# Attention of two blocks: the transposes of a block two steps after its scores, its values three steps after, and six score buffers in place of four

## The chip, the cores and the metric

The kernel runs on one core of a Trainium2 chip. The metric is the device time of one execution in microseconds (us). The engines are named as the profile names them: PE (TensorE, matmuls; PEld is its weight load), DVE (VectorE), ACT (ScalarE), POOL (GpSimd), SP (SyncE, which issues most transfers). L512 is line 512 of the kernel.

## What is computed

Two blocks of two layers each on 512 tokens of width 1024, all in float32. The change lies in the attention of the first layer of either block; the rest (a mixture of experts, a state space mixer, convolutional feed-forward layers) is left as it is. Cut to the two attentions:

```python
def chunk_attention(q, k, v, rel_bias):          # first block, 8 heads of 64
    ...
    scores = jnp.einsum('bclhd,bcshd->bchls', q, k_band).astype(jnp.float32) * (ATT_HEAD_DIM ** -0.5)
    scores = scores + bias[None, None]
    scores = jnp.where(valid[None, :, None, None, :], scores, -1e30)
    p = jax.nn.softmax(scores, axis=-1).astype(v.dtype)
    o = jnp.einsum('bchls,bcshd->bclhd', p, v_band)

def fox_attention(q, k, v, f_logit, q_gain, k_gain):   # second block, 8 heads of 64
    ...
    s = jnp.einsum('bqhd,bkhd->bhqk', qi, k).astype(jnp.float32) * scale
    s = s + ci.transpose(0, 2, 1)[..., None] - ck[:, :, None, :]
    s = jnp.where(kpos[None, :] <= pi[:, None], s, NEG_INF)
    pr = jax.nn.softmax(s, axis=-1)
    return jnp.einsum('bhqk,bkhd->bqhd', pr.astype(v.dtype), v)
```

## The kernel before

Activations lie with channels on the 128 partitions and the 512 tokens along the free axis. A linear layer of 1024 x 128 weights (`lin`, L253) is 24 matmuls of 128x512, since every operand is split into a high and a low part and three products are kept (L268, L269, L270). `flowing` (L308) issues such a layer in two halves of 12 matmuls with a `yield` between; between the halves the kernel puts other matmuls, so that PE has work while the other engines are busy with a softmax. Weights come through SP into `w`; ACT casts them to `wh` (L223), DVE takes the difference `wl` (L224), two buffers each.

Attention is done for a pair of heads at a time, four pairs per block, by the generator `attend` (L501). The queries are cut into four blocks of 128 tokens; block i has 128(i+1) keys.

- `scores(i, h)` (L508): one matmul into a bank of `pa` (two buffers; L512); DVE adds the bias and keeps the maximum (L517), ACT takes the exponential and its sum (L521), DVE takes the reciprocal and scales the row (L522, L523). The result is the tile `S`.
- `turned(i, h)` (L525): i+1 transposes of `S` by PE into a bank of `pm` (L530); ACT copies them to the tile `PT` (L532).
- `values(i)` (L534): 2(i+1) matmuls of `PT` with the values `vt` into `po` (one buffer; L538).

One step of `attend` holds the scores of block j for both heads, then the values of block j-2, then the transposes of block j-1, and a `yield`. There are six steps.

PE's instructions stand in the order in which they are written (a manual schedule); the other engines' order is set by a scheduler that places each instruction by its own estimate. `pm` has two buffers in all, and besides the transposes of `S` they serve the transposes of the value rows (`v_rows`, L494, L498, copied to `vt` by DVE at L499), those of the norms of q and k (`heads`, L1896), the sums of squares (L1882), and in the gated units L1951, whose bank DVE reads at L1959.

In the first block (`mixer0`, L556) a pair's projections v, k, q give six halves, and after each of them one step of the pair before is run; whatever is left is run at the end of the pair (`drain`, L654), before the next pair's first half. At the same time DVE reduces the rows of the modulation weights (`ada`, L419; L441, 128x1024 each), whose tiles `we` SP loads. In the second block (`mixer2`, L1789) `heads` has two steps, in the second of which the first step of `attend` runs, and then one step after each half of the following projections; a pair that is not finished goes on beside the next pair or, for the last one, beside the gated units (`gated`, L1938; `spatial`, L1964). DVE there also computes factors for a later layer (`s5_factors`, L1397; L1407).

Of the kernel before, what the change touches and what calls it, by code (L numbers as in the profile page):

```python
# [17 lines left out]
T = 512  # L18
# [122 lines left out]
def _build(ctx, tc, A, out, dbg, upto, cap):  # L141
    nc = tc.nc
    V, S, G, PE = nc.vector, nc.scalar, nc.gpsimd, nc.tensor
# [10 lines left out]
    def tl(p, shape, tag, bufs=1, dt=F32):  # L154
        return p.tile(list(shape), dt, name=tag, tag=tag, bufs=bufs)
# [6 lines left out]
    def ps_(tag="ps", bufs=3):  # L162
        return tl(pp if tag in ("ps", "pm") else phase["px"], [128, T], tag, bufs)
# [337 lines left out]
    def attend(ap, c, q):  # L501

        qT, kT, vt = q["q"], q["k"], q["vt"]
        sm, pts = {}, {}

        def scores(i, h):  # L508
            w = 128 * (i + 1)
            pb = 64 * h  # L510
            sp = ps_("pa", 2)
            PE.matmul(sp[:, :w], qT[pb:pb + 64, i * 128:w], kT[pb:pb + 64, :w], start=True, stop=True)  # L512
            s = sm[i, h] = tl(ap, [128, T], "S", 4)
            m = tl(ap, [128, 4], "m", 8)
            prev = -3e38
            for n, (c0, c1, b) in enumerate(q["bias"][h](i)):
                V.tensor_tensor_reduce(s[:, c0:c1], sp[:, c0:c1], b, 1.0, prev, op0=ADD, op1=MAX,  # L517
                                       accum_out=m[:, n:n + 1])
                prev = m[:, n:n + 1]
            V.tensor_scalar(m[:, 2:3], prev, -1.0, None, op0=MUL)  # L520
            S.activation(s[:, :w], s[:, :w], AF.Exp, bias=m[:, 2:3], accum_out=m[:, 3:4])  # L521
            V.reciprocal(m[:, 3:4], m[:, 3:4])  # L522
            V.tensor_scalar(s[:, :w], s[:, :w], m[:, 3:4], None, op0=MUL)  # L523

        def turned(i, h):  # L525
            w = 128 * (i + 1)
            s = sm.pop((i, h))
            tp = ps_("pm", 2)
            for j in range(i + 1):
                PE.transpose(tp[:, j * 128:(j + 1) * 128], s[:, j * 128:(j + 1) * 128], ident)  # L530
            pt = pts[i, h] = tl(ap, [128, T], "PT", 4)
            S.activation(pt[:, :w], tp[:, :w], AF.Copy)  # L532

        def values(i):  # L534
            for j in range(i + 1):
                for h in range(2):
                    f = (2 * c + h) * 64
                    PE.matmul(q["o"][64 * h:64 * h + 64, i * 128:(i + 1) * 128], vt[:, j, f:f + 64],  # L538
                              pts[i, h][:, j * 128:(j + 1) * 128], start=(j == 0), stop=(j == i))

        for j in range(6):
            for h in range(2):
                if j < 4:
                    scores(j, h)
            if j == 2:
                q["o"] = ps_("po", 1)
            if j >= 2:
                values(j - 2)
            for h in range(2):
                if 1 <= j < 5:  # L550
                    turned(j - 1, h)
            yield


# [1 line left out]
    def mixer0(rb, mp):  # L556
        with ExitStack() as st:
# [84 lines left out]
            for c in range(5):  # L642
                q = {"vt": vt}
                lins = inner(c, q) if c < 4 else project(0)
                if c < 4:
                    biases(c, q)
                for n, _ in enumerate(lins):
                    if att:
                        step(att)
                    if c == 0 and n < 4:  # L650
                        pooled(n)
                    step(aw, 2 if n % 3 == 0 else 1)
                if att:
                    drain(att)  # L654
                    mixed[3 + c] = hl(op, 16, old["o"])
                if c < 4:
                    att, old = attend(ap, c, q), q
# [1131 lines left out]
    def mixer2(sp, hf):  # L1789

        with ExitStack() as st:
# [98 lines left out]
            def heads(c, q):  # L1890
# [12 lines left out]
                for h in (2 * c, 2 * c + 1):  # L1903
# [10 lines left out]
                    q["bias"].append(bias)  # L1914
                yield
                att = attend(ap, c, q)
                next(att)
                v_rows(q["v"], vt, c)
# [209 lines left out]
```

## Time and profile before

| | |
|---|---|
| median of 3 runs | 2448.61 us (2448.13 to 2453.47) |
| the profiled execution | 2448.66 us, its span 2446.9 us |
| PE, DVE, ACT busy | 95%, 72%, 45% of the span |
| `attend` in the first block | 85.8 to 191.8 us |
| `attend` in the second block | 1228.1 to 1353.3 us |
| transposes L530, values L538 in all | 160 and 320 matmuls |

PE is busy nearly always, so what a stage can win is read from PE's idle time there and from the clock that was granted, not from the shares of the whole span. A row of PE gives the modelled duration of a matmul, which is longer than the distance to the next start, since matmuls are pipelined.

### The profile page before, as it was taken

What the parts mean: (1) busy time and instruction counts of PE and PEld (TensorE: products, weight loads), DVE (VectorE), ACT (ScalarE), POOL (GpSimd) and SP (SyncE); (2) the same over time, 40 slices, a digit from 0 to 9 for tenths busy, and PEclk for the clock granted to TensorE, in tenths of its full rate; (3) what the DMA queues carried; (4) which work ended last, traced back from release to release, by engine and by line L of the source; (5) the groups of instructions that cost most, each with busy time, mean ns of one, the idle gap of its engine ahead of it and who ended that gap; (6) DMA issues with size and microseconds to landing.
All of it is one profiled execution on the core that took longest, in us unless ns stands there. A gap on an engine that the chain in (4) does not pass through costs nothing.

```text
span 2446.9 us, 35789 instructions
## 1 busy us (share of the span) xinstructions
PE 2328.9 (95%) x13173; PEld 1906.3 (78%) x13174; DVE 1750.3 (72%) x3323; ACT 1096.4 (45%) x1750; POOL 486.6 (20%) x498
## 2 busy tenths in 40 slices
PE   7999899899999999999999999999998799999999
PEld 4767799677777776998766777778787788888887
DVE  6985678699996885776686687647847756745755
ACT  3444787434433434885245434324333244423432
POOL 0000444100000002343010394676521000000000
PEclk9999999899999999999899999999999999999999
DMA  9862898553354225896221233343347733323242
GB/s 343 290 214 92 285 334 281 179 186 124 113 165 145 87 77 182 289 338 236 75 70 62 84 118 112 104 132 112 103 129 236 205 106 95 95 84 108 95 126 95
DMA packets 136789, 385.94 MB, mean 158 GB/s; under 512 B 24696, under 2 KB 41208, under 8 KB 134560
## 3 DMA queue, kind: packets, MB, share of 16 engines
q1 hardware_dynamic: 121408, 338.51, 42.0%
q0 software_dynamic: 7552, 26.74, 3.2%
q10 hardware_dynamic: 7648, 18.32, 2.2%
q8 instruction: 108, 1.77, 0.3%
q14 instruction: 73, 0.60, 0.1%
HBM read 354.13 MB, written 29.38 MB: 157 GB/s over the span
## 4 chain that ended last, share of the span: by engine, by line
PE 43%; DVE 7%; ACT 1%; issue 1%; DMA 0%; SPq 0%; POOL 0%; ACTq 0%; DVEq 0%; POOLq 0%
PE ps L268 13%; PE ps L270 13%; PE ps L269 13%; DVE wl L224 2%; DVE hc L2016 1%; ACT wh L223 1%; PE pm L372 0%; PE sk L1590 0%; PE pa L512 0%; DMA w<-w_d 0%; PE pm L530 0%; PE py L1715 0%; PE po L538 0%; DVE hc L2020 0%; PE pm L1580 0%
## 5 line engine op out<-in xcount | busy, mean ns | idle before, releaser
L268 PE MATMUL ps<-hi,wh 128*128 128x512 f32 (+2 forms) x2248 | 899.7, 400 | 4.0 <-ACT hi L485 3.2
L270 PE MATMUL ps<-hi,wl 128*128 128x512 f32 (+2 forms) x2248 | 885.8, 394 | 8.8 <-DVE wl L224 8.8
L269 PE MATMUL ps<-lo,wh 128*128 128x512 f32 (+2 forms) x2248 | 885.6, 394 | 3.7 <-DVE lo L486 2.7
L223 ACT ACTIVATE wh<-w 128x1024 fp32r<-128x1024 f32 (+3 forms) x323 | 306.9, 950 | 572.9 <-PE ps L269 384.6
L224 DVE TENSOR_TENSOR wl<-w,wh 128x1024 fp32r<-128x1024 f32 (+3 forms) x323 | 370.6, 1147 | 215.8 <-ACT wh L223 211.7
L270 PEld LDWEIGHTS ps<-hi,wl 128*128 128x128 f32 (+1 forms) x2248 | 425.3, 189 | 110.1 <-DVE wl L224 13.7
L268 PEld LDWEIGHTS ps<-hi,wh 128*128 128x128 f32 (+1 forms) x2248 | 425.8, 189 | 106.9 <-issue 12.4
L269 PEld LDWEIGHTS ps<-lo,wh 128*128 128x128 f32 (+1 forms) x2248 | 426.1, 190 | 96.0 <-DVE lo L486 4.0
L224 DVE TENSOR_TENSOR wl<-we,wh 128x1024 fp32r<-128x1024 f32 x128 | 173.9, 1373 | 59.9 <-ACT wh L223 55.2
L931 POOL TENSOR_TENSOR hl<-hT,hh 128x1024 fp32r<-128x1024 f32 x60 | 137.1, 2284 | 174.5 <-ACT hh L930 80.9
L223 ACT ACTIVATE wh<-we 128x1024 fp32r<-128x1024 f32 x128 | 136.0, 1064 | 48.7 <-PE pa L949 21.5
L2016 DVE SCALAR_TENSOR_TENSOR hc<-f,cols,hc 128x511 f32<-128x511 f32 (+1 forms) x176 | 152.4, 866 | 6.5 <-ACT hc L2014 3.1
L911 PE MATMUL ps<-ht,w 128*128 128x128 f32 x1024 | 125.7, 276 | 5.1 <-ACT ht L961 5.1
L911 PEld LDWEIGHTS ps<-ht,w 128*128 128x128 f32 x1024 | 119.4, 191 | 7.0 <-ACT ht L961 6.9
L734 POOL IOTA io<- 128x512 f32 x2 | 1.1, 564 | 574.9 <-PE ps L270 574.9
L2012 DVE TENSOR_TENSOR f<-ps,rb 128x512 f32<-128x512 f32 x88 | 60.5, 687 | 68.6 <-PE ps L270 68.3
L441 DVE CUSTOM_DVE_ANT_0 we<-we,crow 128x1024 f32<-128x1024 f32 x80 | 96.5, 1215 | 3.7 <-DMA we<-in_ada_t_dram 3.3
L949 PE MATMUL pa<-wh,hh 128*128 128x256 f32 x496 | 88.4, 300 | 1.0 <-ACT hh L930 1.0
L223 ACT ACTIVATE hi<-hc 128x512 fp32r<-128x512 f32 x44 | 27.8, 632 | 127.7 <-DVE hc L2020 127.7
L491 DVE SCALAR_TENSOR_TENSOR x<-ps,mod,x 128x512 f32<-128x512 f32 x52 | 39.0, 749 | 60.3 <-PE ps L270 50.1
L949 PE MATMUL pa<-wh,hl 128*128 128x256 f32 x496 | 78.8, 280 | 1.4 <-DVE hl L931 1.4
L949 PE MATMUL pa<-wl,hh 128*128 128x256 f32 x496 | 78.6, 280 | 0.0
(571 smaller groups left out, 3252.0 us busy)
## 6 DMA issues: line engine op xcount, KB each, us to landing
we<-in_w_ex_dram SPq DMA_DIRECT2D x128, 512.0 KB, 5.8
w<-in_w_fu_dram SPq DMA_DIRECT2D x88, 512.0 KB, 3.5
we<-in_ada_t_dram SPq DMA_DIRECT2D x80, 512.0 KB, 5.1
w<-in_w_ex_dram SPq DMA_DIRECT2D x64, 512.0 KB, 5.6
w<-in_w_si_dram SPq DMA_DIRECT2D x48, 512.0 KB, 3.5
w<-in_w_fd_dram SPq DMA_DIRECT2D x32, 512.0 KB, 3.7
w<-in_w_ei_dram SPq DMA_DIRECT2D x20, 512.0 KB, 3.5
aw<-in_ada_w_dram SPq DMA_DIRECT2D x16, 512.0 KB, 9.4
```

The source lines that it names most:

```text
L223: S.activation(hi, src, AF.Copy)
L224: eng.tensor_tensor(lo, src, hi.bitcast(F32), op=SUB)
L268: PE.matmul(ps[:m], a, h, start=(not more and k + j == 0), stop=False)
L269: PE.matmul(ps[:m], a, l, start=False, stop=False)
L270: PE.matmul(ps[:m], b, h, start=False, stop=(last and k + j == nk - 1))
L441: V.tensor_tensor_reduce(w, w, row, 1.0, 0.0, op0=MUL, op1=ADD, accum_out=st[:, n:n + 1])
L491: V.scalar_tensor_tensor(xs[c], ps, mod(l, seg, c), xs[c], op0=MUL, op1=ADD)
L911: PE.matmul(p[:, c * 128:(c + 1) * 128], w2[:, (4 * q + c) * 128:(4 * q + c + 1) * 128], hd, start=True, stop=True)
L931: (V if e < 2 else G).tensor_tensor(hl_, win, hh.bitcast(F32), op=SUB)
L949: PE.matmul(hp[:, 0:256], h[:, 4 * n + k], w[:, k * 256:(k + 1) * 256], start=(n + i + k == 0), stop=(n + i + k == 6))
L2012: V.tensor_tensor(t, next(up)[1], rb, op=MUL)
L2016: V.scalar_tensor_tensor(c[:, d:], t[:, :T - d], C(f"fw{l}{2 - d}", n), c[:, d:], op0=MUL, op1=ADD)
```

## The change

The number of `S` buffers goes from four to six. A step of `attend` now holds the scores of block j, the values of block j-3 and the transposes of block j-2, and there are seven steps.

```diff
@@ -510,7 +510,7 @@
             pb = 64 * h
             sp = ps_("pa", 2)
             PE.matmul(sp[:, :w], qT[pb:pb + 64, i * 128:w], kT[pb:pb + 64, :w], start=True, stop=True)
-            s = sm[i, h] = tl(ap, [128, T], "S", 4)
+            s = sm[i, h] = tl(ap, [128, T], "S", 6)
             m = tl(ap, [128, 4], "m", 8)
@@ -538,17 +538,17 @@
-        for j in range(6):
+        for j in range(7):
             for h in range(2):
                 if j < 4:
                     scores(j, h)
-            if j == 2:
+            if j == 3:
                 q["o"] = ps_("po", 1)
-            if j >= 2:
-                values(j - 2)
+            if j >= 3:
+                values(j - 3)
             for h in range(2):
-                if 1 <= j < 5:
-                    turned(j - 1, h)
+                if 2 <= j < 6:
+                    turned(j - 2, h)
             yield
```

PE in `mixer0`, at the end of the first pair (the same for the second and third): the values of block 2 (L538 x6), the transposes of block 3 (L530 x8), and then a half of a projection. Before:

```order
L538 MATMUL po<-PT,vt 64x128 x6
L530 MATMUL pm<-ident,S 128x128 x8
L268 MATMUL ps<-hi,wh 128x512
L269 MATMUL ps<-lo,wh 128x512
L270 MATMUL ps<-hi,wl 128x512
```

With the change, at the same place:

```order
L270 MATMUL ps<-hi,wl 128x512
L538 MATMUL po<-PT,vt 64x128 x6
L530 MATMUL pm<-ident,S 128x128 x8
L538 MATMUL po<-PT,vt 64x128 x8
L268 MATMUL ps<-hi,wh 128x512
```

Before, the twelve matmuls of a half stood between the transposes of block 3 and its values (L538 x8); now the values follow the transposes directly, because `mixer0` has six halves for seven steps.

PE in `mixer2`, at the end of the second pair (the same at the first and third): the next pair's transposes of its norms (`ye`, L1896) come in the same step.

```order
 L538 MATMUL po<-PT,vt 64x128 x6
 L530 MATMUL pm<-ident,S 128x128 x8
+L1896 MATMUL pm<-ident,ye 128x128 x8
 L268 MATMUL ps<-hi,wh 128x512
 L269 MATMUL ps<-lo,wh 128x512
```

Before, L1896 stood a half later, behind the values of block 3; now it follows the transposes of block 3, which fill both banks of `pm`.

PE in `mixer2`, beside the second gated unit: the transposes L1951 now stand ahead of the fourth pair's values of block 2 and transposes of block 3.

```order
+L268 MATMUL ps<-hi,wh 128x512
+L269 MATMUL ps<-lo,wh 128x512
+L270 MATMUL ps<-hi,wl 128x512
+L1951 MATMUL pm<-ident,f 128x128 x4
 L538 MATMUL po<-PT,vt 64x128 x6
 L530 MATMUL pm<-ident,S 128x128 x8
```

L1951 stood ahead of the values of block 3 before; so a bank of `pm` is now held by the gated unit while block 3 is transposed.

## Rows read from the trace of the kernel before

**Rows 1.** The page, busy time, share of the span, instructions of each engine.

```profile
PE 2328.9 (95%) x13173; PEld 1906.3 (78%) x13174; DVE 1750.3 (72%) x3323; ACT 1096.4 (45%) x1750; POOL 486.6 (20%) x498
```

**Rows 2.** Busy time by stretch: PE, PEld, DVE, ACT, POOL; then PE's clock, DMA share, GB/s.

```profile
110.00:140.00 30.00, 28.87 (x173) 20.48 (x173) 27.58 (x75) 15.34 (x34) 0.00 (x0) 1.00 0.91 322
1240.00:1270.00 30.00, 27.61 (x171) 20.62 (x171) 27.64 (x143) 12.86 (x28) 2.97 (x2) 0.99 0.20 57
...
1228.00:1353.00 125.00, 115.92 (x687) 86.26 (x688) 95.64 (x394) 62.62 (x143) 12.43 (x12) 0.97 0.22 68
```

**Rows 3.** Waits of PE in the first block's attention: total, times, longest.

```profile
PE pm L530 <- DVE mod L407: 1.0, 1, 1.0
PE pm L530 <- DVE S L523: 1.0, 1, 1.0
PE pm L530 <- DVE vt L499: 0.5, 1, 0.5
```

**Rows 4.** DVE in the first block: its waits for transfers, and two copies to `vt`.

```profile
DVE we L441 <- DMA we<-in_ada_t_dram: 2.8, 4, 2.0
...
122.41 0.67 DVE L499 COPY vt<-pm 128x512 f32<-128x512 f32 x1
...
151.29 0.68 DVE L499 COPY vt<-pm 128x512 f32<-128x512 f32 x1
```

**Rows 5.** Timeline of PE, end of the first pair: start, duration, what, idle before.

```profile
105.16 0.63 PE L530 MATMUL pm<-ident,S 128*128 128x128 f32 x4
106.76 0.63 PE L530 MATMUL pm<-ident,S 128*128 128x128 f32 x4 [0.97 <-DVE mod L407]
...
110.11 1.09 PE L538 MATMUL po<-PT,vt 128*64 128x128 f32 x16
```

**Rows 6.** Timeline of ACT at the same place.

```profile
105.89 0.60 ACT L532 ACTIVATE PT<-pm 128x512 f32<-128x512 f32 x1 [2.11 <-PE pm L530]
...
109.98 1.06 ACT L223 ACTIVATE wh<-w 128x1024 fp32r<-128x1024 f32 x1 [1.90 <-PE ps L269]
110.95 0.58 ACT L622 ACTIVATE q<-ps 128x512 f32<-128x512 f32 x1
```

**Rows 7.** Waits of PE in the second block's attention.

```profile
PE pm L530 <- DVE m L520: 1.9, 3, 1.0
...
PE po L538 <- ACT PT L532: 1.6, 2, 0.8
PE pm L530 <- DVE m L522: 1.5, 2, 0.8
PE pa L512 <- DVE qk L1899: 1.4, 1, 1.4
PE pa L512 <- DVE m L517: 1.4, 2, 0.7
PE pm L530 <- DVE S L523: 1.1, 2, 0.7
```

**Rows 8.** Timeline of PE: eight transposes L1896, and what follows them.

```profile
1257.93 1.09 PE L1896 MATMUL pm<-ident,ye 128*128 128x128 f32 x8
1258.78 0.47 PE L268 MATMUL ps<-hi,wh 128*128 128x512 f32 x1
```

**Rows 9.** Timeline of PE at two places where its clock falls.

```profile
1237.15 0.63 PE L268 MATMUL ps<-hi,wh 128*128 128x512 f32 x1
...
1331.34 0.33 PE L530 MATMUL pm<-ident,S 128*128 128x128 f32 x1 [0.99 <-DVE m L520]
...
1332.21 0.39 PE L268 MATMUL ps<-hi,wh 128*128 128x512 f32 x1
1332.44 0.40 PE L269 MATMUL ps<-lo,wh 128*128 128x512 f32 x1
...
1333.05 0.63 PE L268 MATMUL ps<-hi,wh 128*128 128x512 f32 x1
1333.48 0.63 PE L269 MATMUL ps<-lo,wh 128*128 128x512 f32 x1
```

## The prediction

> **What bounds the kernel now.** I read the page's busy times first: PE is busy 95% of the span, DVE 72%, ACT 45% [rows 1]. So a stage gives back only what PE idles in it, or runs at half clock. The busy times by stretch show the same inside the two attentions: in 110 to 140 us (first block) PE is busy 28.9 of 30 us at a granted clock of 1.00; in 1240 to 1270 us (second block) 27.6 of 30 at 0.99, with DVE at 27.6 of 30 as well; over the whole second attention, 1228 to 1353, PE at 115.9 of 125 and DVE at 95.6 [rows 2]. The list of PE's waits tells what the idle time was spent on. In the first block it holds little: 1.0 us behind `mod` (L407), 1.0 behind the scaled row `S`, 0.5 behind a copy to `vt` [rows 3]. In the second block transposes (L530) wait 1.9, 1.5 and 1.1 us, seven times in all, for DVE rows of the softmax (L520, L522, L523), values (L538) 1.6 us for ACT's copy `PT`, and scores (L512) 1.4 us for DVE's work on q and k (L1899) and 1.4 us for L517 [rows 7]. Last comes PE's timeline where its clock falls. At full clock a 512 column matmul starts 0.23 us after the one before; from 1333.05 us the distance is 0.43 [rows 9], the lower of the two levels (1.2 for 2.4 GHz). There are two such stretches, from 1237.15 and from 1333.05 us, eight matmuls each, both after a series of waits: 8 x (0.43 - 0.23) = 1.6 us each.
>
> **The change, second block: what it takes away.** The profiled execution took 2448.66 us, the median is 2448.61, so sums against the one hold for the other.
> - The transposes now come a whole half (12 matmuls, 12 x 0.23 = 2.8 us at least) after their block's softmax was to be ready before. The longest wait was 1.0 us, so all are covered: 1.9 + 1.5 + 1.1 = -4.5 us [rows 7].
> - Values wait for `PT` where exponentials stood ahead of the copies on ACT. The copies now have a half of their own and the exponentials are of a block two on: -1.6 us [rows 7].
> - The first scores after the projections wait 1.4 us for L1899 [rows 7]. Now the 16 matmuls of the older pair's values stand ahead of them, by the row of the same 16 matmuls 1.0 us [rows 5], and DVE reaches L1899 a few small operations sooner: -1.2. The 1.4 us for L517 are a matter of the two `pa` banks, which stay as they are: 0.
> - Each wait is longer than its row tells: the matmul before is modelled at 0.40 us but starts are 0.23 apart [rows 9], so some 0.17 us belongs to each of 10 waits: -1.7.
> - Clock. The second fall comes after the wait of 0.99 us at 1331.34 [rows 9], one of the waits that go: -1.6. The first comes after waits for L517, which stay, and for softmax rows, which go; I take half: -0.8.
>
> Sum: -11.4 us.
>
> **The change, second block: what it adds.** The norms' transposes L1896 now stand directly behind the transposes of block 3, which fill both banks of `pm`. They wait for ACT to copy the first bank out. ACT's copy starts 0.73 us after the first of four transposes (105.16 to 105.89) and takes 0.60 [rows 5, 6]: 1.33 us until the bank is free. PE comes to L1896 after eight transposes, and eight take 0.85 us from start to next start (1257.93 to 1258.78) [rows 8]. So 0.5 us, or 0.55 with the signal, three times: +1.6. Queued behind L1896 on PE is the next half of the projections, which needs nothing of it and is late by as much; nothing is queued behind on ACT, whose copies run as they come. From below this wait is nothing (PE arrives late and the copy runs early); from above it is 1.1 us, if one more operation as long as the copy (0.60) stands ahead of it on ACT. Beside the gated units L1951 holds one of the two banks, so transposes of the second head wait for the copy of the first, as at 1331.34 now [rows 9]: I take 0.65 us at the first unit (0.99 less the part that the softmax row was late) and 0.85 at the second, where block 3 is as wide as the bank. Sum: +3.1, between +0.5 and +6. Second block: -11.4 + 3.1 = **-8.3 us**.
>
> **The change, first block.** The waits of [rows 3] go: -2.5, and -0.5 for the part that the modelled ends hide, -3.0 in all. Two costs come.
> - Pair ends. Six halves stand for seven steps, so values of block 3 come directly behind its transposes, where 12 matmuls stood between. ACT there has the cast `wh` (1.06 us), a copy of q (0.58) and then two `PT` copies of 0.60 and some 0.5 [rows 6]. With ACT free, PE would wait for the second copy: 0.73 + 0.60 + 0.5 = 1.83 us from the first transpose, less 0.85 for the eight: 1.0. With the cast just ahead it is 2.0; with the copies started early, 0.6. I take 0.95, nearest to the free case, since the projection's last matmuls end before and its copy is over when the transposes end. Three pair ends: +2.85 (1.8 to 6). Behind the waiting values on PE stands the next pair's first half.
> - DVE. It is busy 27.6 of 30 us here [rows 2] and waits for transfers of `we` [rows 4] while DMA is at 0.91 [rows 2]. PE's lead over DVE cannot grow there: the copies to `vt` come when DVE comes to them (122.41 and 151.29 us) [rows 4], and they hold a `pm` bank that transposes of the old pair need, now of an earlier block, one step sooner. The row of that wait is 0.5 us [rows 3]; for two pairs I take 0.75 each: +1.5 (0 to +3).
>
> First block: -3.0 + 2.85 + 1.5 = **+1.4 us**, from -1 to +4.5. The two buffers more of `S` cost nothing by themselves: they hold rows and issue nothing.
>
> **Sum:** -8.3 + 1.4 = -6.9 us, so 2448.7 - 6.9 = **2441.8 us**; with the bounds 2438.5 to 2443.9 as the likeliest one's own range.
>
> **Rivals.**
> - *Flat.* DVE sets the pace in both blocks. In 1240 to 1270 it is as busy as PE [rows 2], its stream is not shortened by the change, and `pa` and `pm` banks come free only when it has read them. Then the waits of transposes return as waits of scores (L512 behind L517), now 1.4 us [rows 7], and only the clock (-1.6) and the 0.8 of values return to the sum: 2448.7 - 2.4 = 2446.3, with 2444 to 2450 around it. For it: DVE at 27.6. Against: over all of 1228 to 1353 us PE has 20 us more work than DVE (115.9 and 95.6) [rows 2], and DVE's factors for a later layer can slip to where PE doesn't look at them.
> - *Larger gain.* Both falls of the clock go (-0.8 more), the first block's three pair ends cost 1.8 instead of 2.85 and DVE takes nothing back (-1.0 and -1.5), L1896 is half covered (-0.8), and one more `pa` wait goes with the shifted steps (-0.7): 2441.8 - 4.8 = 2437.0, down to 2436.
> - *Slower.* PE's clock falls after a new wait for a bank. The change makes eleven new short waits: three at pair ends in the first block, two or three behind `vt` there, three at L1896, two beside the gated units. A fall costs 1.6 us [rows 9]. With n falls the sum is -6.9 + 1.6 n: from n = 8 it lies above 2453.5 (2448.7 - 6.9 + 12.8 = 2454.6), at all 11 it is 2459.4. For it: both falls stand behind series of waits of 0.7 to 1.4 us. Against: the first block had waits of 1.0 us and kept a clock of 1.00 [rows 2, 3], and of the dozen waits in the second block two series only were followed by a fall.
>
> What a page says against the change: the Trainium skill, "TensorE: Matmul & The Clock Gate", section "A second HAM failure mode: psum-queue depth-cycling", tells of a kernel that went round its PSUM banks and idled PE briefly between groups of matmuls so often that its clock swung between half and full rate. Two `pm` banks filled and waited for in a row are such a place, so by that page the third rival is the natural one. The two falls of [rows 9] agree with it; the waits of [rows 3], after which the clock stayed, do not.
>
> **How the numbers follow.** A difference under 0.2% (4.9 us: 2443.7 to 2453.5) is about what a measurement of this kernel can't tell from no change. Forecast 0.47, which lies almost wholly below 2443.7; larger gain 0.10; flat 0.30, of which a sliver reaches below; slower by the clock 0.13. That gives faster 0.57, same 0.29, slower 0.14 (the slower case and a tail of the first block's upper bounds). The range reaches from the larger gain, 2436, over the forecast to the upper end of the flat case, 2450; left out are the slower case and a little of either tail.
>
> **What would show it.** In the profile after: PE's waits of L530 behind L520, L522 and L523 in the second block gone (right if under 1 us is left of 4.5); L1896 waiting for `PT` three times at about 0.5; no stretch at half clock behind 1331 us; in the first block L538 waiting for `PT` three times at about 1.0 and L530 for `vt` in the second and third pairs. The forecast is wrong if scores (L512) wait as long as the transposes did, if values at the pair ends wait 2 us each, if the whole second block is as long as before while PE's waits moved to another line, or if the granted clock of either attention falls below 0.97.

## The result

The changed kernel takes 2432.03 us (median of 6 runs, 2430.55 to 2439.54) where the kernel before takes 2448.37 (6 runs, 2442.14 to 2453.47). The ratio is 0.9942 with a 95% interval from 0.9925 to 0.9958: 14.2 us less (10.3 to 18.4); the two medians differ by 16.3. The forecast was 2441.8, its range 2436 to 2450; faster was right, the size was not, and the result lies below the range. The profiled execution of the changed kernel took 2439.54 us, 9.1 less than the profiled one before, and was the longest of its six. So its trace holds less of the gain than the runs do, and both need an explanation.

The page of the changed kernel (busy time, share, instructions), and busy time by stretch as in [rows 2]; the second and third stretch lie in the second attention:

```profile
PE 2331.8 (96%) x13173; PEld 1908.3 (78%) x13174; DVE 1750.8 (72%) x3323; ACT 1094.6 (45%) x1750; POOL 486.1 (20%) x498
```

```profile
110.00:140.00 30.00, 29.63 (x166) 20.99 (x164) 28.18 (x77) 13.79 (x32) 0.00 (x0) 1.00 0.89 313
1240.00:1270.00 30.00, 29.69 (x184) 22.38 (x182) 28.57 (x147) 13.18 (x30) 2.86 (x2) 1.00 0.21 71
1228.00:1353.00 125.00, 121.46 (x728) 91.06 (x727) 98.24 (x407) 66.47 (x151) 12.13 (x12) 1.00 0.22 70
```

In 1240 to 1270 us PE now does 184 instructions where it did 171, and is busy 29.7 of 30 us in place of 27.6. DVE is at 28.6 and does not hold it up. The clock is 1.00 throughout: both half-clock stretches of [rows 9] are gone from this execution.

What PE waits for in the changed kernel (total, times, longest), in the first attention (85 to 192 us):

```profile
PE po L538 <- ACT PT L532: 1.2, 3, 0.6
```

and around the second (1215 to 1353 us):

```profile
PE pm L1838 <- DVE s_sn L1423: 1.9, 1, 1.9
PE pa L512 <- DVE m L517: 1.5, 2, 0.8
PE pm L530 <- ACT PT L532: 1.1, 2, 0.7
PE pm L1896 <- ACT PT L532: 0.9, 3, 0.3
PE pm L1896 <- DVE f L1850: 0.3, 1, 0.3
```

No transposes wait for a softmax any more; all lines of [rows 3] are gone, and of [rows 7] all but L517. What came are waits for ACT's copies `PT`, at eight of the places that were forecast, in all 3.2 us of idle time. L1838 and the wait of L1896 for L1850 are in the kernel before, too.

The timeline of PE shows the three kinds: the end of a pair in the first block, L1896, and the transposes beside the gated units (start, duration, what, idle before):

```profile
106.66 1.09 PE L530 MATMUL pm<-ident,S 128*128 128x128 f32 x8
108.06 1.58 PE L538 MATMUL po<-PT,vt 128*64 128x128 f32 x16 [0.31 <-ACT PT L532]
```

```profile
1253.56 1.14 PE L1896 MATMUL pm<-ident,ye 128*128 128x128 f32 x8 [0.31 <-ACT PT L532]
```

```profile
1325.83 0.33 PE L530 MATMUL pm<-ident,S 128*128 128x128 f32 x1 [0.37 <-ACT PT L532]
...
1341.36 0.66 PE L530 MATMUL pm<-ident,S 128*128 128x128 f32 x4 [0.75 <-ACT PT L532]
```

**One measure for all kernels.** To compare profiles, I take the time between the same two matmuls in each: from the projection ahead of the attention to one behind it (before: 84.05 to 221.96 and 1229.23 to 1372.93 us). The rows of the second attention before and after (busy time of the engines, clock, DMA share, GB/s):

```profile
1229.23:1372.93 143.70, 134.62 (x773) 101.77 (x771) 107.75 (x426) 70.06 (x162) 12.43 (x12) 0.98 0.21 65
```

```profile
1227.86:1362.67 134.81, 131.27 (x772) 99.18 (x771) 105.47 (x426) 69.97 (x162) 12.13 (x12) 1.00 0.22 69
```

A stretch at half clock costs 1.6 us, as worked out from [rows 9]. So 143.7 with two such stretches is 140.5 without them, and 134.8 has none: 5.7 us less, and the waits of PE in it fall by 5.6. The table has this for every profiled execution of a whole kernel; the labels are those of the experiments below.

| kernel | first attention | second | its half-clock stretches | second without them |
|---|---|---|---|---|
| before | 137.9 | 143.7 | 2 | 140.5 |
| before, again (e1) | 138.6 | 142.0 | 1 | 140.4 |
| six S alone (e10) | 138.9 | 143.9 | 2 | 140.7 |
| empty step (e9) | 138.4 | 143.5 | 2 | 140.3 |
| first block alone (e4) | 138.3 | 143.8 | 2 | 140.6 |
| changed | 137.1 | 134.8 | 0 | 134.8 |
| changed, again (e2) | 138.7 | 136.4 | 1 | 134.8 |
| changed, four S (e5) | 136.8 | 135.1 | 0 | 135.1 |
| changed, carried (e11) | 135.2 | 134.8 | 0 | 134.8 |
| second block alone (e3) | 139.0 | 138.0 | 2 | 134.8 |
| values late (e6) | 137.7 | 137.6 | 1 | 136.0 |
| first pair alone (e7) | 138.3 | 140.3 | 1 | 138.7 |
| pairs 2 to 4 (e8) | 138.8 | 138.2 | 1 | 136.6 |
| transposes late (e12) | 138.7 | 151.8 | 3 | 147.0 |

The last column repeats within 0.4 us from one execution to the next. The first attention scatters by a microsecond: the nine kernels with the old order there have 138.5 on average, the four with the change alone 137.7; the standard error of this difference is 0.5.

### The profile page after: what moved, and what is told of

Same layout as the page of the kernel before. It is cut to its first block, busy times and chain, and to the rows that moved or that the text cites. A ratio compares the mean times of both kernels' runs of the same rounds, so it can differ in the third digit from the quotient of the medians.

```text
span 2437.8 us, 35781 instructions
## 1 busy us (share of the span) xinstructions
PE 2331.8 (96%) x13173; PEld 1908.3 (78%) x13174; DVE 1750.8 (72%) x3323; ACT 1094.6 (45%) x1750; POOL 486.1 (20%) x498
## 4 chain that ended last, share of the span: by engine, by line
PE 44%; DVE 6%; ACT 1%; issue 1%; DMA 0%; SPq 0%; POOL 0%; ACTq 0%; POOLq 0%; DVEq 0%
PE ps L268 13%; PE ps L270 13%; PE ps L269 13%; DVE wl L224 2%; DVE hc L2016 1%; ACT wh L223 1%; PE pa L512 0%; PE po L538 0%; PE pm L530 0%; PE sk L1590 0%; PE py L1715 0%; DMA w<-w_d 0%; PE pm L372 0%; DVE hc L2020 0%; PE pm L1580 0%
## 5 line engine op out<-in xcount | busy, mean ns | idle before, releaser
L931 POOL TENSOR_TENSOR hl<-hT,hh 128x1024 fp32r<-128x1024 f32 x60 | 138.5, 2308 | 174.0 <-ACT hh L930 98.0
L441 DVE CUSTOM_DVE_ANT_0 we<-we,crow 128x1024 f32<-128x1024 f32 x80 | 96.2, 1215 | 1.4 <-DMA we<-in_ada_t_dram 1.2
```

The lines of the kernel that those rows point to most:

```text
L441: V.tensor_tensor_reduce(w, w, row, 1.0, 0.0, op0=MUL, op1=ADD, accum_out=st[:, n:n + 1])
L931: (V if e < 2 else G).tensor_tensor(hl_, win, hh.bitcast(F32), op=SUB)
```

## The experiments

### Again, and one block at a time

`e1` is the kernel before, `e2` the changed one. In `e3` and `e4` the change is made for one block alone, by a parameter that sets the two delays, the number of steps and the number of `S` buffers (cut to the calls):

```diff
-    def attend(ap, c, q):
+    def attend(ap, c, q, lag=2):
@@ e3, in mixer0
-                    att, old = attend(ap, c, q), q
+                    att, old = attend(ap, c, q, 1), q
@@ e4, in mixer2
-                att = attend(ap, c, q)
+                att = attend(ap, c, q, 1)
```

> The kernel before, unchanged, for a second profile and for the spread of its times. Two theories of why the median of the change fell by 14 us or more where the two profiles show only 9.5 us in the two attentions and nothing in sum elsewhere. A: the stretches at half clock in other places differ from one execution to the next, and the profiled execution of the changed kernel had more of them than its other runs; then this profile has its half-clock stretches partly at other places than the first one, with times spread over about 10 us, ratio 1.000 within 0.002. B: stretches are fixed to places in the program, and the change removed some of them for good; then this profile repeats the first one's 18 stretches at the same instructions, and the times stay within 3 us of each other.

> The changed kernel, unchanged, for a second profile. A: ratio 0.994 within 0.002; its second profile has fewer or other half-clock stretches outside the attentions than the first one (the one from 231.8 us among the likely to be gone), and the two attentions alone are shorter than before by 9 to 10 us again. B: the same stretches as in the first profile, 231.8, 433, 1559 and 1709 us among them, and about the same time as that one, 2439.

> The change in the second block alone; the first block's attention is as before, with four S buffers. By the prediction's sum this gives -8.3 us (2440); by the alignment of the two profiles -8.9 in the attention itself; with the clock's part under theory A up to -13 (2435 to 2440). Rival: the gain beyond the forecast comes from the first block, then no more than -8 here (2440 or more).

> The change in the first block alone. By the prediction's sum +1.4 us (2450); by the alignment of the two profiles -0.7 (2448). Rival: the first block brings what the sum lacks, by clock or otherwise, then -5 us or more (2443 or less). In its profile values of block 3 wait for PT three times, 1.2 us in all as in the changed kernel, against 2.85 us in the prediction.

Measured, as ratios to the kernel before: e1 1.0002 (0.9984 to 1.0021), e2 0.9942 (0.9920 to 0.9964), e3 0.9941 (0.9925 to 0.9957), e4 0.9987 (0.9974 to 1.0001). The change in the second block brings all that can be measured; for the first alone the interval reaches no change.

Theory A holds in its main part: the kernel before, run again, takes 2442.98 to 2457.45 us, and its profile has some half-clock stretches at other places than the first one, in layers that the change doesn't touch (one from 234.6 us that the first lacks, none from 612.5 where the first has one). Theory B falls by this spread. But what A expected of the second profile of the changed kernel did not come: it took 2448.04 us, the longest of its six runs, has as many half-clock stretches as the first, among them all four that B named, and its two attentions are only 6.5 us shorter than before, not 9 to 10. Part of the long time is something else (last section). So the stretches fall at a set of places that returns, of which each execution has a part. The times of the kernel before scatter with a standard deviation of some 5 us.

In `e2` and `e4` the wait for `vt` that was forecast for the first block comes up (1.5 and 1.1 us), while the first profile of the changed kernel has none of it. The waits of `e2` in the first attention:

```profile
PE pm L530 <- DVE vt L499: 1.5, 2, 1.1
PE po L538 <- ACT PT L532: 1.2, 3, 0.6
```

### Which part of the change does it

```diff
@@ e5: four buffers, the changed order
-            s = sm[i, h] = tl(ap, [128, T], "S", 6)
+            s = sm[i, h] = tl(ap, [128, T], "S", 4)
@@ e6: second block alone, values late, transposes as before
             if j >= 3:
                 values(j - 3)
             for h in range(2):
-                if 2 <= j < 6:
-                    turned(j - 2, h)
+                if 1 <= j < 5:
+                    turned(j - 1, h)
@@ e12: second block alone, six steps; transposes late, values directly after
+            if j >= 2:
+                turned(j - 2, 0)
+                turned(j - 2, 1)
             for h in range(2):
                 if j < 4:
                     scores(j, h)
...
+            if j >= 2:
+                values(j - 2)
```

> The changed order in both blocks with four S buffers as before. The forecast held that the two buffers more cost and bring nothing by themselves; but with four, the rows of block j may only be written when the transposes of block j-2 are over, which now stand behind the scores of block j on PE. Theory: DVE's softmax of each block starts later, by the scores, the values and the transposes of one step (0.9 + 0.4 + 0.7 us or so), and about half of the gain is lost (2440 to 2445). Rival: DVE is late anyway, then 2435 as with six.

> In the second block alone, values three steps after their scores but transposes one step after, as before (S with six buffers, first block as before). By the sum's terms: the 1.6 us of values behind PT and the 1.2 us behind L1899 are saved, the 4.5 us of transposes behind the softmax stay, and so do the clock's falls: -3 us (2446), 2441 or less if the values are what makes the gain.

> In the second block alone, transposes two steps after their scores and values in the same step, with the next scores between them; six steps, first block as before. Values late alone made the profiled second attention 4.5 us shorter (free of half-clock stretches), both together 5.7. If the transposes' waits of 4.5 us were worth as much by themselves, this gives -4.5 less what the values now wait for PT (0.7 to 1.0 us, eight to sixteen times, 3 blocks of them with scores between): the attention about the same as before or up to 5 us longer. Rival, that the waits of transposes alone matter: 4 us shorter.

Measured: e5 0.9948 (0.9932 to 0.9964), e6 0.9946 (0.9931 to 0.9961), e12 1.0021 (1.0006 to 1.0035). For e5 the rival holds, and for e6 the alternative of 2441 or less (2437.43). For e12 the attention became longer than expected. With four buffers nothing is lost: 135.1 us in the second attention for 134.8, so DVE does not need the other two. Values late alone bring 4.5 of the 5.7 us (136.0 for 140.5), not 3. Transposes late without the values cost 6.5 us (147.0 for 140.5), somewhat more than the 5 that were the upper end. What PE waits for in `e6` around the second attention:

```profile
PE pa L512 <- DVE m L517: 1.5, 2, 0.8
PE pm L530 <- DVE m L522: 1.1, 2, 0.7
PE pm L530 <- DVE s_t L1407: 0.8, 2, 0.6
PE pm L530 <- ACT PT L532: 0.6, 1, 0.6
PE pm L530 <- DVE S L523: 0.6, 1, 0.6
PE pm L530 <- DVE m L520: 0.4, 1, 0.4
...
```

and in `e12`:

```profile
PE po L538 <- ACT PT L532: 6.3, 9, 2.1
PE pm L530 <- ACT PT L532: 2.8, 3, 1.3
PE pa L512 <- DVE m L517: 1.5, 2, 0.8
```

In `e6` the waits of values (1.6 us) and of the first scores (1.4) of [rows 7] are gone, and of the 4.5 us of the transposes 2.9 are left behind the softmax and DVE's small operations, though the transposes were not moved. Why they wait less was not tested by itself; at a pair's start the last values of the older pair now stand ahead of the first scores, so PE comes to these transposes later. The second step of lag then saves the 2.9 and pays with 0.9 at L1896 and 0.5 more beside the gated units. In `e12` the softmax is covered as well, but values wait nine times for the copy of their own transposes, up to 2.1 us. The rows of waits, 10.6 us for 9.1 before, show only a small part of the 6.5 us. The rest is in the values themselves, which run as the two heads' copies come; the sixteen records of block 3 take 1.50 us to the next start, where they took 1.02 (1256.91 to 1257.93 us in the kernel before; L1899 is its L1896):

```profile
1244.99 1.57 PE L538 MATMUL po<-PT,vt 128*64 128x128 f32 x16 [0.31 <-ACT PT L532]
1246.49 1.09 PE L1899 MATMUL pm<-ident,ye 128*128 128x128 f32 x8
```

Over all values of the second attention that makes some 5 us.

### One pair, and what is common to all

```diff
@@ e7: second block, the first pair alone (e8: the other three alone)
-                att = attend(ap, c, q)
+                att = attend(ap, c, q, *((1, 2) if c else (2, 3)))
@@ e9: the kernel before, in the second block with a step that does nothing
-        for j in range(6):
+        for j in range(7):
...
-            if j >= 2:
+            if 2 <= j < 6:
                 values(j - 2)
@@ e10: the kernel before
-            s = sm[i, h] = tl(ap, [128, T], "S", 4)
+            s = sm[i, h] = tl(ap, [128, T], "S", 6)
```

> The second block's change for its first pair of heads alone, the other three pairs as before. Aligned by their matmuls, the two profiles win 3.2 us over this pair, 1.6 of it by the half-clock stretch from 1237 us. Theory of waits: -3 us (2446). Rival, that the granted clock of the timed executions (0.979 before, 0.982 after) hangs on this stretch with its four waits in a row: -8 us or more (2441 or less), with a mean granted clock near 0.982.

> The second block's change for the second, third and fourth pair, the first as before. Aligned by their matmuls, the two profiles win 5.7 us over these, 1.6 of it by the half-clock stretch from 1333 us. Theory of waits: -6 us (2443). If the clock hangs on the first pair: not more than that, clock 0.980. If on these: -10 or more, clock 0.982.

> The kernel before, with a seventh step in the second block's attention that does nothing. Every run with another order in the second block was some 7 us faster in its timed executions than its profiled second attention (free of half-clock stretches) is shorter, whichever part was changed. What they have in common is one more step for a pair: it moves the scalings of x (L1927) and with them DVE's small operations, the order on PE stays as before. Theory D (the step and DVE's order bring the 7 us): 2442 to 2444 against 2449 to 2451, granted clock 0.982. Theory W (PE's waits bring it): same as before within 3 us, clock 0.979.

> The kernel before with six S buffers in place of four, in both blocks: no instruction moves on any engine, only addresses. The forecast: 0. Rival: where tiles lie moves the time by some us, then 2442 to 2446.

Measured: e7 0.9962 (0.9947 to 0.9976), e8 0.9951 (0.9934 to 0.9967), e9 1.0005 (0.9991 to 1.0019), e10 0.9990 (0.9974 to 1.0006). The two buffers alone and the step alone bring nothing that can be measured, so theory D falls, and so does a gain by where tiles lie. Of e7 and e8 either gained in its runs what was expected if the clock hangs on its part, which can't be true of both (9.3 and 12.0 us); the 3 and 6 us of the theory of waits are too little for either.

In the windows the parts add up: 1.8 us for the first pair, 3.9 for the others, 5.7 together. The run times seem not to: 9.3 and 12.0 us, for 14.5 together (`e3`, on another chip); with errors of some 2 us each this alone decides nothing. But nearly all runs with another order on PE in the second block are shorter, by some 5 us, than their windows and the missing half-clock stretches account for; `e11`, 11.7 us less by its means where its windows give 10.9, is the exception. The runs' mean granted clock goes with it in most: 0.979, 0.977 and 0.980 for the kernel before on the chips of these three groups, 0.979 to 0.980 for e1, e4, e9 and e10, and 0.980 to 0.983 for e2, e3, e5 to e8, e11 and e12. On the chip of `e9` to `e12` the difference is small: 0.981 for `e11`, which has the fewest waits of these, and for `e12`, which has the most, against 0.980, a difference of 0.001 with an error near 0.0007. So the number of waits does not tell it here. The profiled executions have nothing of it: their clock is 0.980 on average for the five kernels with the old order in the second block, and 0.980 for the eight of the table with its change or a part of it, e12 aside. In five of these eight (changed, e2, e3, e7, e8) the profiled execution was the longest of its runs.

### Where the rest arises

`e13` and `e14` are the kernels before and after, ended behind the second attention's layer; `e15` and `e16`, ended behind the first block; `e17` and `e18` have the second attention's layer alone, six times.

```diff
@@ e17, e18: in place of all layers
+    for _ in range(6):
+        with ExitStack() as b2:
+            hf = pool(b2, "hf")
+            sm = tl(fp, [128, 8], "sums", 1)
+            V.memset(sm, 100.0)
+            summed.append(lambda sm=sm: sm)
+            mixer2(pool(b2, "s5par"), hf)
+            sofar.clear()
```

> The kernel before, ending after the layer with the second attention (everything behind it is left out; x is written out as it stands). About 1430 us. It is the measure for the next one.

> The changed kernel, ending after the layer with the second attention (everything behind it is left out). If the 5 us that the profiles don't account for arise in the second attention itself, it is 13 to 15 us shorter than its counterpart of the kernel before. If they arise in stages behind it (by where the clock falls there), it is 7 to 9 us shorter, as the profiled attentions say (5.7 and 0.7 without half-clock stretches, 1.7 with them).

> The kernel before, ending after the first block (the whole second block is left out). About 1210 us. It is the measure for the next one.

> The changed kernel, ending after the first block (the whole second block is left out). By the profiled attentions 0.7 us shorter than its counterpart of the kernel before, by the prediction 1.4 us longer; if the missing 5 us arise in the first block, 5 to 6 us shorter.

> The layer with the second attention of the kernel before, six times in a row on the input x; all other layers are left out, and the sums of squares that it takes from the layer ahead are a constant. Some 6 x 235 us. It is the measure for the next one.

> The layer with the second attention of the changed kernel, six times in a row on the input x; all other layers are left out, and the sums of squares that it takes from the layer ahead are a constant. If the layer is worth what the profiled executions show (5.7 us of waits and some 1.7 of clock a time), it is 34 us shorter without the clock and 44 with it. If the missing 5 us arise in this layer, 65 us or more, most of the surplus by a higher mean granted clock.

Measured (medians of 5 runs each): behind the layer 1427.47 and 1416.95 us, 10.5 less (the means 11.1, with a standard error of 2.6); behind the first block 1179.69 and 1177.44, 2.3 less (the means 1.7, error 1.8); six times the layer 1451.89 and 1412.58, 39.3 less (the means 38.1, error 1.5). The first pair lies between its two expectations and decides nothing; the second speaks against 5 to 6 us in the first block, at about two errors.

The last pair is the sharp one: 38.1 / 6 = 6.4 us a time, which excludes 11. What PE waits for in the attentions of `e17`, all six together:

```profile
...
PE po L538 <- ACT PT L532: 15.0, 17, 1.5
PE pm L530 <- DVE m L520: 14.4, 16, 1.1
...
PE pm L530 <- DVE S L523: 7.1, 17, 0.8
PE pm L530 <- DVE m L522: 5.8, 8, 1.0
PE pa L512 <- DVE m L517: 5.7, 6, 1.2
```

and in `e18`:

```profile
...
PE pm L530 <- ACT PT L532: 6.7, 12, 0.7
PE pa L512 <- DVE m L517: 6.5, 6, 1.4
PE pm L1896 <- ACT PT L532: 5.6, 18, 0.3
```

48.0 us of waits became 18.8: 29.2 of the 38.1, or 4.9 a time. The rest goes with the mean granted clock, 0.978 and 0.983: the product of a run's span and its granted clock, an estimate of its time at full clock, falls by 30.4 us (error 1.1), so the waits are nearly all of it. The same product falls by 6.0 (error 1.0) from `e13` to `e14`, about what the waits are worth there, and the other 5 or so of their 11.1 us go with the clock. So the layer itself is worth 6 to 7 us, 5 of them by waits that the profile names. The remainder of the 14.2, some 5 us, can be put to none of the three places: not to this layer when it runs by itself, 1.7 +- 1.8 in the first block, and 14.2 - 10.5 = 4 with an error near 4 behind the layer. It goes with a higher clock in the runs, and the profiled executions don't show at which stretches. **Where it arises stays open.**

### A version beyond the change

In `e11` the seventh step of a pair in the first block stands behind the first half of the next pair:

```diff
                 for n, _ in enumerate(lins):
+                    if rest:
+                        drain(rest[0])
+                        mixed[2 + c] = hl(op, 16, rest[1]["o"])
+                        rest = None
                     if att:
                         step(att)
...
-                if att:
+                if att and c < 4:
+                    rest = att, old
+                elif att:
                     drain(att)
```

> The changed kernel, and in the first block the last step of a pair (values of block 3) stands behind the first half of the next pair instead of directly behind the transposes of block 3. The 1.2 us that these values wait for PT in the changed kernel's profile should go, with some 0.5 that the modelled ends hide: -1.7 us against the changed kernel, so 2432 to 2436, if DVE doesn't take it back at vt; then the same as the changed kernel.

Measured: 0.9954 (0.9935 to 0.9973), 2435.84 us. Its first attention is 135.2 us, 2.5 below the mean of the four with the change. The waits in it:

```profile
PE pm L530 <- DVE vt L499: 1.1, 1, 1.1
PE pm L530 <- ACT PT L532: 0.4, 1, 0.4
```

The waits of values for `PT` are gone; their cost seems to be larger than the 1.7 us expected, since they also stretch the values (see the first block below). DVE takes back a part at `vt`. That it beats the changed kernel over the whole cannot be told at this scatter.

## The prediction, step by step

**Waits taken away in the second block.** All three kinds went as forecast (4.5 and 1.6 us, and 1.4 where 1.2 was taken), and L517 stayed (1.4 and 1.5). The term for the modelled ends, -1.7, was wrong: the waits of the attention go from 9.1 us ([rows 7] and 0.2 at L1407) to 3.5, that is by 5.6, and the window without half-clock stretches gets 5.7 shorter. In sum nothing is hidden beside the rows here; where values run as their own copies come, as in `e12`, much is, but in the length of the values and not at the end of the matmul before.

**Waits added there.** 0.9 us at L1896 where 1.6 was taken, 1.1 beside the gated units (0.37 and 0.75) where 1.5 was. In all 2.0 where 3.1 was taken. So the sum without clock, forecast at -5.9 (-7.3 - 1.7 + 3.1), was 5.7: right by terms that were off against each other.

**Clock there.** -2.4 was forecast: by the table 1.8 stretches on average in the five kernels with the old order, 0.6 in the five with the new order in the second block (changed, e2, e3, e5, e11), 1.9 us less.

**First block.** +1.4 was forecast, the windows have -0.8 (error 0.5), so the sign was most likely wrong. The pair ends are not the reason. Values idle only 0.31, 0.31 and 0.59 us before they start, but then the sixteen records of these values take 1.58 us where they took 1.09 [rows 5]: the first needs the first head's copy alone, the second waits for the other. That is 0.8, 0.8 and 1.1 us, 2.7 for 2.85 forecast, and `e11`, which takes this away, is 2.5 us shorter. ACT's rows at the first of these places, where the copies start 0.75 us after the first transpose and end at 108.50:

```profile
105.72 1.06 ACT L223 ACTIVATE wh<-w 128x1024 fp32r<-128x1024 f32 x1 [1.95 <-PE ps L269]
106.69 0.58 ACT L622 ACTIVATE q<-ps 128x512 f32<-128x512 f32 x1
107.41 1.09 ACT L532 ACTIVATE PT<-pm 128x512 f32<-128x512 f32 x2
```

The terms that were off are the other two. The waits taken away are 3.0 us in the first profile (with two short lines that [rows 3] leaves out), but 3.1 to 4.4 in eight more with the old order there, 3.6 on average of all nine, and -3.0 was taken, 0.5 of it for modelled ends. The cost at `vt`, taken at 1.5, was 1.5 and 1.1 in `e2` and `e4` and nothing in the first profile after and in `e5`: 0.65 on average. With these, -3.6 + 2.7 + 0.65 is -0.3, within its error of the -0.8.

**The sum.** By the windows -5.7 - 1.9 - 0.8 = -8.4 us, where -6.9 was forecast: 2440.3 from the profiled execution, inside the range. The step that failed is the sentence that sums against the profiled execution hold for the median because the two times agree, and with it the term *Clock*: it priced two stretches of one execution at -2.4 and put the clock of all other stretches, and of all other executions, at nothing without a reason. The runs showed in its place a mean granted clock of 0.980 to 0.983 for the kernels with a changed second block, where the kernel before had 0.977 to 0.980. On the chips of `e2` and `e3` and of `e5` to `e8` that is 0.003 or more, by estimate some 7 us of 2440, and the surplus over the windows is some 5 us. Why the clock rises, and at which stretches, stays open. The other wrong terms, the modelled ends and the first block, moved the forecast by some 2 us each, in opposite directions. The range was built from the cases alone; with no term for the scatter of the runs it was too narrow below. Its inner bounds, 2438.5 to 2443.9, do not follow from the bounds given for the blocks either (-10.9 to -5.4 and -1 to +4.5), which add up to 2436.8 to 2447.8.

**The rivals.** *Flat* is out: DVE is at 28.6 of 30 and PE is not held, and scores wait as long as before (1.5 for 1.4). *Slower* is out: eight new waits are in the first profile after, and the clock stayed at 1.00 in both attentions. The section cited from the Trainium skill, "TensorE: Matmul & The Clock Gate" ("A second HAM failure mode: psum-queue depth-cycling"), tells of a clock that swings after brief idle times between groups of matmuls. The first profile of the changed kernel, whose eight waits are of that kind, does not show it; `e12`, which idles PE most (10.6 us of waits) and has three half-clock stretches in its second attention, the most of the table, agrees. *Larger gain* (2437.0) came nearest; of its terms the two falls of the clock and nothing taken back at `vt` came true in the first profile, and the cheap L1896 in all, but not cheaper pair ends nor the `pa` wait (L517 stayed). That it lies nearest to the median is luck: the surplus is none of its terms.

## What to carry to other kernels

Where PE waits in turn for a softmax and for the copy of its own transposes, move the last user first: values one step later brought most of the gain in the second attention here (4.5 of 5.7 us), transposes one step later without them a loss. Judge such a change by the time between the same two matmuls in both traces, less the stretches at half clock; that repeated within 0.4 us where whole runs scatter by some 5 us. It tells what the waits are worth; a third of what the runs gained here was not in it. And give a forecast of a few microseconds in a long kernel a term for that scatter, from several runs, before its range is set.

## What the runs showed of the hardware that was not expected

In the profile of `e2`, matmuls start 0.267 us apart from 719.5 to 771 us, not 0.233, though the granted clock is 1.00. In no other profile of these kernels does this stretch have it. PE's timeline where it begins, and the counts of matmuls by stretch:

```profile
719.30 0.39 PE L270 MATMUL ps<-hi,wl 128*128 128x512 f32 x1
719.53 0.42 PE L268 MATMUL ps<-hi,wh 128*128 128x512 f32 x1
719.79 0.43 PE L269 MATMUL ps<-lo,wh 128*128 128x512 f32 x1
720.05 0.43 PE L270 MATMUL ps<-hi,wl 128*128 128x512 f32 x1
720.32 0.43 PE L268 MATMUL ps<-hi,wh 128*128 128x512 f32 x1
```

```profile
719.00:745.00 26.00, 26.00 (x98) 18.87 (x99) 23.87 (x37) 4.86 (x5) 0.00 (x0) 1.00 0.76 248
745.00:771.00 26.00, 26.00 (x100) 18.72 (x99) 8.19 (x11) 4.23 (x4) 0.00 (x0) 1.00 0.44 157
771.00:780.00 9.00, 9.00 (x59) 6.96 (x59) 6.62 (x14) 3.99 (x6) 0.00 (x0) 1.00 0.17 58
```

Some 194 matmuls with 0.034 us more each are 6.6 us, and nothing in the row of the clock tells of it. What causes it was not tested.
